# Fourier channels of the last prompt rows ahead of three products of the preceding rows, and the mixing steps with them

## The chip, the cores and the metric

The kernel runs on one core of a Trainium2 chip. The metric is the device time in microseconds of one execution. PE is TensorE, ACT is ScalarE, DVE is VectorE, POOL is GpSimd, SP is SyncE, which here only issues DMA transfers.

## The reference

One layer of a bidirectional encoder over a prompt of 2048 rows and a sample of 256, both with d_model 1024, each with a memory of 256 rows:

```python
h = rmsnorm(x, g_mix)
proj = h @ w_in                      # [q 512 | k 128 | v 128 | fourier 256 | memory q 256]
q, k, v, uf, qm = jnp.split(proj, [o1, o2, o3, o4], axis=-1)
y_attn = window_gqa_attention(q, k, v, sinks)      # |t-s| <= 128, ALiBi, sink
y_four = fourier_mix(uf)                           # real part of the 2-D DFT over rows and channels
y_mem = memory_cross_attention(qm, rmsnorm(mem, g_mem), w_mem_kv)
x = x + group_output_norm(y_attn, y_four, y_mem, g_grp) @ w_out
hf = rmsnorm(x, g_ffn) @ w_ff1                     # then squared ReLU, @ w_ff2, residual, final norm
```

The Fourier mixing needs all rows of a sequence, so its last part can only begin when the Fourier channels of the last prompt rows (rows 1792 to 2047) are there.

## The kernel before, in words

Float32 operands are split into a high and a low part (`hi_of` on ACT, L103; `lo_of` mostly on DVE, L106), and each product is three matmuls (L100).

**First stage: the input projection.** The rows go in nine groups of 256, x0 to x8 (x8 is the sample), with the two memory groups m0 and m1 between. A group is normalised (`norm`), transposed and split (`transposed`, tiles `hh` and `hl`), and multiplied in five products, `pj_g_mp`, of 48 matmuls each: mp 3 gives the Fourier channels, 2 the keys and values, 0, 1 and 4 the queries. Keys, values and queries are written to Kd, Vd and Qd in DRAM. Behind mp 3 comes `channel_mix`: the DFT over channels and, from x4 on, sums and differences with earlier rows. Norm and transposes of the next group stand at mp 1 and 4. `w2_work`, sums of rows of w_ff2 on POOL, is stepped in groups 2 to 6; what is left of it, and the ALiBi table (`bias_table`), come ahead of group 6.

**The mixing** is the generator `fourier()`. After a first `yield` and a setup it makes eleven tiles, in the order 0, 8, 4, 2, 6, 1, 7, 3, 5 (prompt) and 9, 10 (sample, which need x8's channels). For each tile a table `seq` of 256 KB is loaded on POOL's queue (L458), six matmuls give `po` (`spectrum`), and one step later `spread` evacuates and scales it (L497 to L508, with two POOL instructions at L134 and L135) and stores it to Y or Z in DRAM (L510): on ACT's queue up to the seventh tile, on POOL's from there. `mirror(1)` on ACT's queue and `mirror(0)` on POOL's (L486) copy Z to the mirrored rows of Y, 512 KB each. The generator is stepped by group 7 (once per product from the second on) and group 8 (twice per product).

**Second stage: attention and output projection.** Blocks of 128 rows go in pairs. SP loads the ALiBi table (L633), keys `kb` (L643), queries `qb` (L649), values `vb` (L651) of a pair, memory keys `km` (L663) and values `vm` (L668), the mixed channels `y` (L778), and the eight slabs of w_out (`wos`, L833), which ACT and DVE scale and split into `woh` (L170) and `wol` (L171). Scores `s` and `sm`, exponentials `p` (L684) and `pm` (L699), transposes `t`, `tm` and `ty`, products `ot` and `otm`, and the output projection `op` follow. Then comes the MLP, from about 545 us on.

**What sets the order.** The program is written in the order of the steps above, and a scheduler of the tile framework then orders the instructions of each engine; each engine works through its own in order. SP's transfers wait for buffers, for data in DRAM, and for the landing of an earlier transfer that used the same one of eight completion counters (ACT's and SP's queues share them). SP holds everything behind a transfer that waits. The second stage's buffers lie over those of the first: that of `vm` over the last tile's `fbig`, whose store must have landed. `wos` has three buffers, shared with `xr`, and its order among the transfers is kept as the scheduler first puts it (`keep_in_program_order`).

The lines that the change and the prediction touch:

```python
seq = fpool.tile([P, 2, 2, P], F32R, tag="seq", bufs=2, name=f"seq_{ti}")      # L457
pool.dma_start(seq, seq_d[ti])                                                  # L458
```

Of the kernel before, what the change touches and what calls it, by code (L numbers as in the profile page):

```python
# [11 lines left out]
F32 = mybir.dt.float32  # L12
F32R = mybir.dt.float32r
# [80 lines left out]
def trunk(ctx, tc, x, mem, w_in, w_mem, w_out, w1, w2, gains, g_final, sinks, ident_d, dist_d, cdft_d, seq_d, y):  # L94
# [52 lines left out]
    if True:  # L147
# [7 lines left out]
        wl0 = fpool.tile([P, 4, 512], F32R, name="wl0")  # L155
# [17 lines left out]
        def transposed(xs, name):  # L173
            hh, hl = [], []
            for kp in range(KT // 2):
# [8 lines left out]
                h = apool.tile([P, 2, 2, P], F32R, tag="hT", bufs=11, name=f"hh_{name}_{kp}")  # L184
                l = apool.tile([P, 2, 2, P], F32R, tag="hT", bufs=11, name=f"hl_{name}_{kp}")
# [196 lines left out]
        def group(g, side=None):  # L382
            it = order.index(f"x{g}")
            hh, hl = ready.pop(it)
            fetch(it + 2)
            post = None
            for mp in (3, 2, 0, 1, 4):
                if g == 1:
                    for k in {3: (0,), 2: (1, 2), 0: (3, 4), 1: (5, 6), 4: (7,)}[mp]:
                        load_wmem(k)  # L390
                if mp == 1:
                    norm_item(it + 1)
                if mp == 4:
                    transpose_item(it + 1)
                ps = psm.tile([P, 2, 256], F32, tag="m", name=f"pj_{g}_{mp}")
                for j in range(2):
                    m = 2 * mp + j
                    proj_T(ps[:, j], winc(0, m), winc(1, m), hh, hl)
                if post:
                    post()  # L400
                    post = None
                if mp == 3:
                    xg = None
                    if g >= 4:
                        xg = X1() if g == 8 else fpool.tile([P, 2, 2 * P], F32, tag="xg", bufs=1, name=f"xg_{g}")
                    u = [apool.tile([P, 2, 256], F32R, tag=f"u{c}", bufs=1, name=f"u{c}_{g}") for c in "hl"]
                    hi_of(u[0], ps)
                    lo_of(u[1], ps, u[0])
                    post = lambda u=u, xg=xg: channel_mix(g, u, xg)
                elif mp == 2:  # L410
                    vT = apool.tile([P, 256], F32, tag="vT", bufs=1, name=f"vT_{g}")
                    act.activation(vT, ps[:, 1], AF.Copy)
                    kt = apool.tile([P, 2, 2, P], F32R, tag="Ks", bufs=1, name=f"ks_{g}")
                    kps = ps[:, 0].rearrange("p (b t) -> p b t", b=2)
                    hi_of(kt[:, :, 0], kps)
                    lo_of(kt[:, :, 1], kps, kt[:, :, 0])
                    for dup in range(2):
                        for kv in range(2):
                            sp.dma_start(Kd[2 * g:2 * g + 2, dup * HD:(dup + 1) * HD, kv].rearrange("b p l t -> p b (l t)").bitcast(F32),
                                         kt[kv * HD:(kv + 1) * HD].rearrange("p b l t -> p b (l t)").bitcast(F32))  # L420
                    post = lambda vT=vT: values(g, vT)
                else:
                    q = apool.tile([P, 2, 2, 2, P], F32R, tag="Qs", bufs=2, name=f"q_{g}_{mp}")
                    qv = q.rearrange("p b j e t -> p e j b t")
                    pv = ps.rearrange("p j (b t) -> p j b t", b=2)
                    for e in range(2):
                        a = slice(e * HD, (e + 1) * HD)
                        for j in range(2):
                            act.activation(qv[a, e, j], pv[a, j], AF.Copy, scale=-0.125)
# [1084 lines left out]
```

## Time and profile before

| | |
|---|---|
| time, median of three runs | 2290.38 us (2289.64 to 2291.95) |
| the profiled execution | 2291.58 us, of it 2289.8 us span |
| PE busy in the span | 2205.5 us (96%) |
| DVE, ACT, POOL busy | 1643.4, 1020.2, 853.7 us |
| last matmul of the input projection ends | 351.66 us |
| first matmul of the last mixing tile, of the scores, of the output projection | 356.61, 360.33, 398.75 us |
| DMA from 350 to 362 us | 410 GB/s, busy share 1.05 |

The span runs from the first to the last instruction of the program; what lies around it is 1.8 us. Times inside are counted from the span's start. A row of a timeline has start and duration, engine, line, operation, output<-input, and in brackets the idle time ahead of it and what ended it. SPq, ACTq and POOLq rows are the issue of a transfer; the time to its landing is in the list of DMA issues. The clock is TensorE's granted clock, 1.00 at full speed.

### The profile page before, as it was taken

How to read it: one execution, taken by the hardware profiler on the slowest of the kernel's cores; microseconds unless marked ns; L12 is line 12 of the kernel's file. 1: busy time of each engine (PE TensorE's matmuls, PEld its weight loads, DVE VectorE, ACT ScalarE, POOL GpSimd, SP SyncE). 2: the span in 40 equal slices, each digit the busy share in tenths (PEclk: the TensorE clock that was granted, in tenths of full speed). 3: DMA queues.
4: the chain of work that ended last, by engine and by line, in shares of the span. 5: the costliest groups of instructions: out<-in, count | busy, mean ns of one | idle time of the engine just before them, and what ended most of it. 6: DMA issues, size and time to landing. Idle time of an engine off the chain costs nothing.

```text
span 2289.8 us, 35730 instructions
## 1 busy us (share of the span) xinstructions
PE 2205.5 (96%) x12464; PEld 1999.1 (87%) x12464; DVE 1643.4 (72%) x2962; ACT 1020.2 (45%) x2382; POOL 853.7 (37%) x821
## 2 busy tenths in 40 slices
PE   7999997999999989999999999999999999999997
PEld 7999996888888869889989889899988989999995
DVE  7334467776676758898898876877768876766688
ACT  6333357776667755444444433232224343323223
POOL 3555032014100047887786561411331421111143
PEclk9999998999999999999999999999999999999999
DMA  9987339345544368776677767856798676556563
GB/s 300 320 294 278 99 111 340 127 143 165 166 142 141 106 247 280 264 266 231 227 243 245 272 214 253 270 184 194 253 333 286 189 263 192 188 186 187 193 228 136
DMA packets 213415, 501.15 MB, mean 219 GB/s; under 512 B 20819, under 2 KB 66019, under 8 KB 210931
## 3 DMA queue, kind: packets, MB, share of 16 engines
q1 hardware_dynamic: 199872, 456.20, 59.9%
q0 software_dynamic: 10096, 39.04, 4.7%
q10 hardware_dynamic: 3267, 3.62, 0.5%
q8 instruction: 98, 1.61, 0.3%
q14 instruction: 82, 0.67, 0.1%
HBM read 345.17 MB, written 154.53 MB: 218 GB/s over the span
## 4 chain that ended last, share of the span: by engine, by line
PE 66%; DVE 6%; DMA 5%; POOL 3%; issue 2%; ACT 2%; SPq 0%; ACTq 0%; POOLq 0%; DVEq 0%
PE y L100 24%; PE op L100 8%; PE pc L100 7%; PE pa L100 7%; PE pb L100 7%; PE pd L100 4%; PE ot L100 2%; PE s L100 1%; PE t L707 1%; DMA w1s<-W1D 1%; DVE XTl L106 1%; PE yl L100 1%; DVE acc L333 1%; DMA Xn<-xr 1%; PE sm L100 1%
## 5 line engine op out<-in xcount | busy, mean ns | idle before, releaser
L100 PE MATMUL y<-w2l,ah 128*128 128x512 f32 x966 | 379.0, 392 | 5.9 <-POOL w2l L106 3.4
L100 PE MATMUL y<-w2h,al 128*128 128x512 f32 x966 | 378.8, 393 | 0.0
L100 PE MATMUL y<-w2h,ah 128*128 128x512 f32 x966 | 343.5, 393 | 1.6 <-DVE acc L336 0.9
L103 ACT ACTIVATE ah<-m 128x384 fp32r<-128x384 f32 x238 | 124.6, 524 | 491.0 <-PE y L100 485.0
L106 DVE TENSOR_TENSOR al<-m,ah 128x384 fp32r<-128x384 f32 x238 | 164.8, 693 | 156.0 <-ACT ah L103 154.2
L333 DVE TENSOR_TENSOR acc<-acc,y 128x512 f32<-128x512 f32 x378 | 240.2, 680 | 29.4 <-PE y L100 27.8
L100 PE MATMUL pc<-XTh,w1s 128*128 128x384 f32 x768 | 221.2, 341 | 10.1 <-DMA w1s<-W1D 5.4
L100 PE MATMUL pa<-XTh,w1s 128*128 128x384 f32 x768 | 219.2, 336 | 2.1 <-ACT m L1156 1.1
L100 PE MATMUL pb<-XTh,w1s 128*128 128x384 f32 x768 | 217.6, 336 | 0.9 <-DVE m L333 0.8
L100 PEld LDWEIGHTS y<-w2h,al 128*128 128x128 f32 x966 | 181.5, 188 | 30.1
L100 PEld LDWEIGHTS y<-w2l,ah 128*128 128x128 f32 x966 | 181.6, 188 | 29.6 <-POOL w2l L106 6.2
L100 PE MATMUL pj<-hl_x,winh 128*128 128x256 f32 x720 | 206.2, 288 | 0.0
L100 PEld LDWEIGHTS y<-w2h,ah 128*128 128x128 f32 x966 | 181.1, 188 | 26.3 <-DVE acc L333 1.7
L100 PE MATMUL pj<-hh_x,winl 128*128 128x256 f32 x720 | 204.0, 285 | 0.0
L100 PE MATMUL pj<-hh_x,winh 128*128 128x256 f32 x720 | 201.3, 287 | 1.1 <-ACT hh_x L103 1.1
L103 ACT ACTIVATE w2h<-w 128x512 fp32r<-128x512 f32 x322 | 198.5, 617 | 3.3 <-DMA w1s<-W1D 2.1
L106 POOL TENSOR_TENSOR w2l<-w,w2h 128x512 fp32r<-128x512 f32 x112 | 169.7, 1522 | 71.5 <-ACT w2h L103 69.4
L1028 POOL TENSOR_TENSOR ms<-m,m 128x384 f32<-128x384 f32 x48 | 59.1, 1231 | 297.1 <-DVE m L1135 215.6
L1135 DVE SCALAR_TENSOR_TENSOR m<-m 128x384 f32<-128x384 f32 x192 | 151.5, 789 | 19.3 <-ACT m L1162 17.1
L106 DVE TENSOR_TENSOR w2l<-w,w2h 128x512 fp32r<-128x512 f32 x210 | 162.0, 771 | 3.7 <-DMA W2D<-w2l 3.7
L100 PEld LDWEIGHTS pc<-XTh,w1s 128*128 128x128 f32 x768 | 143.5, 191 | 20.8 <-DMA w1s<-W1D 6.6
L100 PEld LDWEIGHTS pa<-XTh,w1s 128*128 128x128 f32 x768 | 141.3, 188 | 11.7 <-ACT m L1156 1.4
(272 smaller groups left out, 5428.2 us busy)
## 6 DMA issues: line engine op xcount, KB each, us to landing
w1s<-W1D SPq DMA_DIRECT2D x217, 512.0 KB, 4.0
W1D<-w1s SPq DMA_DIRECT2D x112, 512.0 KB, 4.0
w<-in_w_dram SPq DMA_DIRECT2D x206, 256.0 KB, 4.0
w<-W2T SPq DMA_DIRECT2D x184, 256.0 KB, 3.7
w2r<-in_w_dram SPq DMA_DIRECT2D x16, 1024.0 KB, 7.8
W2T<-w2r POOLq DMA_DIRECT2D x16, 1024.0 KB, 6.8
XTl<-Xn SPq DMA_DIRECT2D x21, 768.0 KB, 7.2
qb<-Qd SPq DMA_DIRECT2D x18, 768.0 KB, 6.8
```

The source lines that it names most:

```text
L100: pe.matmul(out, lhsT, rhs, start=start, stop=stop, skip_group_check=more)
L103: act.activation(out, src, AF.Copy, scale=scale)
L106: (eng or dve).tensor_tensor(out=out, in0=src, in1=hi.bitcast(F32), op=ALU.subtract)
L333: TT(out=o, in0=a, in1=b, op=ALU.add)
L707: pe.transpose(t[:, j], p[:, j * P:(j + 1) * P], ident)
L1028: pool.tensor_tensor(out=o, in0=a, in1=b, op=op)
L1135: dve.scalar_tensor_tensor(out=r, in0=r, scalar=0.0, in1=r, op0=ALU.max, op1=ALU.mult)
```

## The change

The product mp 3 of x7 is computed right behind mp 3 and 2 of x6, ahead of x6's 0, 1 and 4; norm and transposes of x7 come earlier, at x6's mp 3 and 2. From there on the mixing generator is stepped once per product, through x6's last three and x7's other four, then twice per product in x8. For this, `group` is split into `begin` and `part`; x7's four `hh` tiles go to a buffer of their own (it had been w_mem's `wl0`, with its later uses ended), `hT` has 12 buffers for 11, and the `seq` tables lie in turn in `seq` (one buffer for two) and in `xg`'s buffer. The ALiBi table and the rest of `w2_work` come behind x6's mp 3 and not ahead of x6.

```diff
-        wl0 = fpool.tile([P, 4, 512], F32R, name="wl0")
+        def spare(name):
+            return fpool.tile([P, 4, 512], F32R, tag="wl0", bufs=1, name=name)
+
+        wl0 = spare("wl0")
...
+            hs = spare("hh_x7") if name == "x7" else None
...
-                h = apool.tile([P, 2, 2, P], F32R, tag="hT", bufs=11, name=f"hh_{name}_{kp}")
-                l = apool.tile([P, 2, 2, P], F32R, tag="hT", bufs=11, name=f"hl_{name}_{kp}")
+                h = (apool.tile([P, 2, 2, P], F32R, tag="hT", bufs=12, name=f"hh_{name}_{kp}") if hs is None
+                     else hs[:, kp].rearrange("p (j b t) -> p j b t", j=2, b=2))
+                l = apool.tile([P, 2, 2, P], F32R, tag="hT", bufs=12, name=f"hl_{name}_{kp}")
...
+        def part(g, mp, side=None):
+            it = order.index(f"x{g}")
+            hh, hl = rows[g]
+            if g == 1:
+                for k in {3: (0,), 2: (1, 2), 0: (3, 4), 1: (5, 6), 4: (7,)}[mp]:
+                    load_wmem(k)
+            if mp == (3 if g == 6 else 1):
+                norm_item(it + 1)
+            if mp == (2 if g == 6 else 4):
+                transpose_item(it + 1)
+            ps = psm.tile([P, 2, 256], F32, tag="m", name=f"pj_{g}_{mp}")
+            for j in range(2):
+                m = 2 * mp + j
+                proj_T(ps[:, j], winc(0, m), winc(1, m), hh, hl)
+            if todo:
+                todo.pop()()
+            if mp == 3:
+                xg = None
...
+                todo.append(lambda: channel_mix(g, u, xg))
...
+            if 2 <= g < 6 or (g, mp) == (6, 3):
+                next(w2_work, None)
+                next(w2_work, None)
+            if side is not None:
+                for _ in range(2 if g == 8 else 1):
+                    next(side, None)
+
+        def group(g):
+            begin(g)
             for mp in (3, 2, 0, 1, 4):
...
-                if 2 <= g < 7:
-                    next(w2_work, None)
-                    next(w2_work, None)
-                if side is not None and not (g == 7 and mp == 3):
-                    next(side, None)
-                    if g == 8:
-                        next(side, None)
...
-            seq = fpool.tile([P, 2, 2, P], F32R, tag="seq", bufs=2, name=f"seq_{ti}")
+            seq = fpool.tile([P, 2, 2, P], F32R, tag="xg" if turn[0] % 2 else "seq", bufs=1, name=f"seq_{ti}")
...
-            elif g < 7:
+            elif g < 6:
                 if g == 3:
                     fe, fab, ffg = f8("fe"), f8("fab"), f8("ffg")
-                if g == 6:
-                    for _ in w2_work:
-                        pass
-                    bias_table()
                 group(g)
         side = fourier()
-        group(7, side)
-        group(8, side)
+        begin(6)
+        part(6, 3)
+        for _ in w2_work:
+            pass
+        bias_table()
+        part(6, 2)
+
+        begin(7)
+        part(7, 3)
+        for g, mps in ((6, (0, 1, 4)), (7, (2, 0, 1, 4))):
+            for mp in mps:
+                part(g, mp, side)
+        begin(8)
+        for mp in (3, 2, 0, 1, 4):
+            part(8, mp, side)
         for _ in side:
             pass
```

The scheduler turns this into another order on each engine. PE at the end of the products, before: `pj_4` is the last product of x8, `po_4313` is tile 10, `s` the first scores.

```order
L100 MATMUL pj_4_4343<-hh_x_3_3743,winh_220 128x256
L100 MATMUL pj_4_4343<-hl_x_3_3744,winh_220 128x256
L100 MATMUL pj_4_4343<-hh_x_3_3743,winl_221 128x256
L100 MATMUL po_4313<-Mh_4309,seq_4307 128x2x66
L100 MATMUL po_4313<-Ml_4310,seq_4307 128x2x66
L100 MATMUL po_4313<-Mh_4309,seq_4307 128x2x66
L100 MATMUL po_4313<-Mh_4309,seq_4307 128x2x62
L100 MATMUL po_4313<-Ml_4310,seq_4307 128x2x62
L100 MATMUL po_4313<-Mh_4309,seq_4307 128x2x62
L100 MATMUL s_0_4470<-kb_4458,qb_4461 128x256 x2
L100 MATMUL s_1_4526<-kb_4458,qb_4461 128x256 x2
```

After, the same tile (`po_4251`) at its new place, behind the transposes of x8's values; `pj_1` is the last but one product of x8.

```order
L100 MATMUL pj_0_4178<-hl_x_3_3833,winh_224 128x256
L100 MATMUL pj_0_4178<-hh_x_3_3832,winl_225 128x256
L380 MATMUL pv_4228<-ident,vT_4108 128x128 x2
L100 MATMUL po_4251<-Mh_4247,seq_4245 128x2x66
L100 MATMUL po_4251<-Ml_4248,seq_4245 128x2x66
L100 MATMUL po_4251<-Mh_4247,seq_4245 128x2x66
L100 MATMUL po_4251<-Mh_4247,seq_4245 128x2x62
L100 MATMUL po_4251<-Ml_4248,seq_4245 128x2x62
L100 MATMUL po_4251<-Mh_4247,seq_4245 128x2x62
L100 MATMUL pj_1_4281<-hh_x_0_3805,winl_223 128x256
L100 MATMUL pj_1_4281<-hh_x_0_3805,winh_222 128x256
```

Tile 10 moved from the end of the products to the start of the last but one; two products now follow it.

SP from the first value block to the fourth slab of w_out, before (`kb_4617`, `qb_4620` and `vb_4619` belong to the second pair of blocks):

```order
L651 DMA vb_4460<-Vd 128x3x256
L649 DMA qb_4465<-Qd 128x1536
L663 DMA km_4468<-Kmd 128x2048
L833 DMA wos_4492<-in_w_out_dram 128x1024
L833 DMA wos_4496<-in_w_out_dram 128x1024
L833 DMA wos_4500<-in_w_out_dram 128x1024
L668 DMA vm_4524<-Vmd 128x1024
L643 DMA kb_4617<-Kd 128x4x512
L649 DMA qb_4620<-Qd 128x1536
L651 DMA vb_4619<-Vd 128x4x256
L778 DMA y_4668<-Yd_72 128x256
L833 DMA wos_4504<-in_w_out_dram 128x1024
```

After (`kb_4614`, `qb_4617` and `vb_4616` are those of the second pair):

```order
L672 DMA vb_4457<-Vd 128x3x256
L670 DMA qb_4462<-Qd 128x1536
L684 DMA km_4465<-Kmd 128x2048
L689 DMA vm_4521<-Vmd 128x1024
L664 DMA kb_4614<-Kd 128x4x512
L670 DMA qb_4617<-Qd 128x1536
L672 DMA vb_4616<-Vd 128x4x256
L854 DMA wos_4489<-in_w_out_dram 128x1024
L854 DMA wos_4493<-in_w_out_dram 128x1024
L854 DMA wos_4497<-in_w_out_dram 128x1024
L799 DMA y_4665<-Yd_72 128x256
L854 DMA wos_4501<-in_w_out_dram 128x1024
```

The first three slabs moved behind `vm` and the three loads of the second pair.

ACT ahead of the first slab, before (`pth` are evacuated transposes of the exponentials):

```order
L684 ACTIVATE p_5_4553,stats_4464<-p_5_4553,stats_4464 128x256
L103 ACTIVATE pth_4_4613<-t_4_4610 128x2x128
L684 ACTIVATE p_6_4566,stats_4464<-p_6_4566,stats_4464 128x256
L103 ACTIVATE pth_4_4613<-t_5_4637 128x2x128
L684 ACTIVATE p_7_4577,stats_4464<-p_7_4577,stats_4464 128x256
L762 ACTIVATE stats_4464<-stats_4464 128x4
L103 ACTIVATE pth_4_4613<-t_6_4652 128x2x128
L170 ACTIVATE woh_4490<-wos_4492,gain 128x1024
L699 ACTIVATE pm_0_4586,stats_4464<-sm_0_4585,stats_4464 128x256
L729 ACTIVATE ots_0_4662<-ot_0_4657 128x512
```

After:

```order
L103 ACTIVATE pth_0_4556<-t_2_4577 128x2x128
L103 ACTIVATE pth_0_4556<-t_3_4592 128x2x128
L720 ACTIVATE pm_0_4583,stats_4461<-sm_0_4582,stats_4461 128x256
L103 ACTIVATE pth_4_4610<-t_4_4607 128x2x128
L705 ACTIVATE p_7_4574,stats_4461<-p_7_4574,stats_4461 128x256
L103 ACTIVATE pth_4_4610<-t_5_4634 128x2x128
L173 ACTIVATE woh_4487<-wos_4489,gain 128x1024
L783 ACTIVATE stats_4461<-stats_4461 128x4
L720 ACTIVATE pm_0_4583,stats_4464<-sm_0_4582,stats_4464 128x256
L173 ACTIVATE woh_4485<-wos_4493,gain 128x1024
```

The first `woh` stands among the same kinds of rows in both, with one exponential of the memory heads (`pm`) now ahead of it.

More of the change, by code (lines that the diff above doesn't have):

```diff
@@ L380, in values, with begin @@
                          vt.rearrange("p b v l d -> p b (v l d)").bitcast(F32))
-        def group(g, side=None):
+        rows, todo = {}, []
+        def begin(g):
             it = order.index(f"x{g}")
-            hh, hl = ready.pop(it)
+            rows[g] = ready.pop(it)
             fetch(it + 2)
-            post = None
-            for mp in (3, 2, 0, 1, 4):
[L388 to L429, printed above, removed]
-                    for e in range(2):
-                        a = slice(e * HD, (e + 1) * HD)
-                        o = slice((1 - e) * HD, (2 - e) * HD)
-                        for j in range(2):
-                            dve.scalar_tensor_tensor(out=qv[o, e, j], in0=pv[a, j], scalar=-0.125,
-                                                     in1=qv[a, e, j].bitcast(F32), op0=ALU.mult, op1=ALU.subtract)
-                    h0 = {0: 0, 1: 4, 4: 8}[mp]
-                    (pool if g == 8 else sp).dma_start(
-                        Qd[2 * g:2 * g + 2, :, h0:h0 + 4].rearrange("b p h t -> p b (h t)").bitcast(F32),
-                        q.rearrange("p b j e t -> p b (j e t)").bitcast(F32))
-                if 2 <= g < 7:
-                    next(w2_work, None)
-                    next(w2_work, None)
-                if side is not None and not (g == 7 and mp == 3):
-                    next(side, None)
-                    if g == 8:
-                        next(side, None)
@@ L448, in trunk @@
+        def group(g):
+            begin(g)
+            for mp in (3, 2, 0, 1, 4):
+                part(g, mp)
         fbig, turn, place_of = [], [0], {}
```

35 lines of the change are left out of this document (added).

## The prediction

> **What bounds the kernel now.** First the page. TensorE (PE) is busy almost all the time, so what a change in the order is worth must be looked for in the few places where PE is not busy.
>
> ```profile
> PE 2205.5 (96%) x12464; PEld 1999.1 (87%) x12464; DVE 1643.4 (72%) x2962; ACT 1020.2 (45%) x2382; POOL 853.7 (37%) x821
> ```
>
> The stretches around the change (start:end, length, busy us of each engine, granted clock, DMA share, GB/s) show where they are.
>
> ```profile
> 230.00:300.00 70.00, 70.00 (x592) 70.00 (x591) 28.83 (x58) 22.11 (x53) 2.96 (x8) 1.00 0.30 91
> 350.00:362.00 12.00, 4.68 (x25) 4.06 (x25) 4.80 (x18) 4.57 (x17) 5.79 (x12) 0.77 1.05 410
> 362.00:372.00 10.00, 7.93 (x41) 6.24 (x40) 7.37 (x30) 8.71 (x31) 2.42 (x4) 0.77 0.92 346
> 372.00:382.00 10.00, 9.24 (x42) 7.67 (x43) 8.05 (x17) 7.90 (x24) 0.00 (x0) 0.66 0.93 340
> 382.00:396.00 14.00, 10.66 (x64) 8.77 (x64) 13.56 (x39) 13.88 (x36) 0.74 (x2) 0.93 0.90 331
> 400.00:540.00 140.00, 138.10 (x830) 120.32 (x829) 102.65 (x278) 102.34 (x293) 22.41 (x41) 1.00 0.42 138
> ```
>
> The products are bound by PE without a gap: 70.00 of 70 us in the first row. From 400 on PE is the bound again (138.10 of 140). In between lie 50 us in which it is not: first the DMA is full (share 1.05), then ScalarE (ACT) is busy 13.88 of 14 us. The PE timeline gives the first gap.
>
> ```profile
> 351.38 0.28 PE L100 MATMUL pj<-hh_x,winl 128*128 128x256 f32 x1
> 356.61 0.45 PE L100 MATMUL po<-Mh,seq 128*128 128x132 f32 x1 [4.95 <-DMA seq<-in_seq_dram]
> 360.33 1.19 PE L100 MATMUL s<-kb,qb 128*128 128x256 f32 x4 [2.21 <-DMA qb<-Qd]
> ```
>
> The last product ends at 351.66. Then PE waits 4.95 us for the table of the last mixing tile, multiplies it, and waits 2.21 us for the first query block. The chain of waits says what follows, read here to the first matmul of the output projection:
>
> ```profile
> 348.38 8.09 DMA seq<-in_seq_dram
> ...
> 363.17 0.59 ACT p L684 x2
> ...
> 369.92 0.44 ACT woh L170
> ...
> 379.54 6.28 DMA wos<-in_w_out_dram
> ...
> 391.85 1.29 DVE wol L171
> ...
> 398.75 0.47 PE op L100 x2
> ```
>
> So before the output projection can start, ACT must split eight slabs of w_out (woh), among the exponentials. In this stretch the time is decided on ACT, not on PE.
>
> **The change, part by part.** *The work.* Nothing is added or removed: the same products, mixing tiles and splits. The x7 Fourier product moves ahead of three x6 products, and the mixing steps start three products earlier, so the six matmuls of the last tile (po of tile 10) now stand ahead of two whole products, 96 matmuls at 0.12 us (the spacing of the pj rows), 11.5 us.
>
> *The early part.* The norms of x4 to x7 move a little against the rest. One small wait of before, for a normalised row block, should go; its row:
>
> ```profile
> 214.01 0.44 PE L183 MATMUL tp_x<-ident,x 128*128 128x128 f32 x2 [1.33 <-DVE x L167]
> ```
>
> New small waits may come: tile 8's table now waits for a buffer shared with xg_7, and the mirror copy on ACT's queue stands ahead of the last split of x8. The gain is at most 1.33; a loss is bounded by two waits of that size, 2.7. I take -0.6 (from -1.3 to +2.0).
>
> *The end of the products.* The 4.95 us wait goes. Products end at 351.66 + 0.7 (six matmuls now inside, at no more than 0.12 each) = 352.4. If tile 10's table (8.09 us in the row above) is still late, PE waits inside the products: its buffer is released by tile 5, some 35 product matmuls and tile 9's own six, about 5 us, ahead of po, so up to 3.1 us. What is late next is the first query block. Its loads and those behind it, from the SP timeline and the list of DMA issues between 343 and 375 us (count, KB each, median us to landing):
>
> ```profile
> 343.21 0.41 SPq L633 DMA_DIRECT2D bias<-Bd  x1
> 343.71 0.41 SPq L643 DMA_DIRECT2D kb<-Kd  x1
> 348.75 0.33 SPq L649 DMA_DIRECT2D qb<-Qd  x1
> 354.78 0.51 SPq L663 DMA_DIRECT2D km<-Kmd  x1
> 356.37 3.17 SPq L833 DMA_DIRECT2D wos<-in_w_out_dram  x3
> 370.18 0.33 SPq L668 DMA_DIRECT2D vm<-Vmd  x1
> 379.12 0.32 SPq L778 DMA_DIRECT2D y<-Yd  x1
> 379.54 1.32 SPq L833 DMA_DIRECT2D wos<-in_w_out_dram  x3
> ```
>
> ```profile
> Qd<-q POOLq DMA_DIRECT2D x3, 512.0 KB, 8.2
> wos<-in_w_out_dram SPq DMA_DIRECT2D x3, 512.0 KB, 12.6
> km<-Kmd SPq DMA_DIRECT2D x1, 1024.0 KB, 11.7
> kb<-Kd SPq DMA_DIRECT2D x1, 768.0 KB, 14.7
> Yd<-Zd POOLq DMA_DIRECT2D x1, 512.0 KB, 12.4
> Vd<-vs SPq DMA_DIRECT2D x1, 256.0 KB, 6.1
> ```
>
> SP works in order behind the Vd write of x8, which stays after its product, so bias goes at about 344, much as before. The query block's DMA waited in before until the first mirror copy, which used the same one of SP's and ACT's eight completion counters, had landed (348.75); that copy is now early, so it goes at about 345.2 and, at the 11.6 us it took (348.75 to 360.33), lands at about 357. The exponentials, which began at 363.17 behind the spread of tile 10, could begin near 359. That would be the gain, some 4 us, if nothing else held ACT.
>
> *What SP does next.* Something else does. In before vm and everything behind it stood until 370.18, because vm's buffer was freed by the store of tile 10, issued here:
>
> ```profile
> 363.56 0.62 POOL L510 DMA_DIRECT2D Yd<-fbig  x1 [0.84 <-ACT fbig L508]
> ```
>
> The scheduler had put the first three slabs of w_out in front of that wait, so they went at 356.37 and the first landed 12.6 later, at 369.0; ACT came to it at 369.92 and did not wait. Now the store comes some 17 us earlier, and the order on SP is vm, kb_2, qb_2, vb_2 (the second pair of blocks) and only then wos_0. By their shapes these four are 512 + 1024 + 768 + 512 = 2816 KB, and in before the transfers of one queue landed in the order of issue (kb 358.4, qb 360.3, km 366.5, wos 369.0). ACT works in order too: its first woh stands behind 16 rows from the first exponential on (17 before, 6.75 us from 363.17), and queued behind it are the exponentials, the copies and the sums that PE and VectorE need. So when wos_0 lands decides when all of them go on.
>
> The price comes from the bytes. What the DMA moved, in the same columns as above, ahead of and after the end of the products:
>
> ```profile
> 343.20:369.00 25.80, 17.56 (x114) 15.86 (x113) 13.80 (x53) 14.69 (x56) 11.07 (x21) 0.80 1.02 377
> 351.00:369.00 18.00, 9.76 (x48) 8.06 (x47) 8.73 (x37) 10.17 (x39) 7.48 (x14) 0.72 1.04 414
> ```
>
> Before, from bias to the landing of wos_0: 25.8 us at 377 GB/s, 9.73 MB. By the issues, in KB: SP 5248 up to wos_0 (Vd 256, bias 768, kb 768, two qb 1536, vb 384, km 1024, wos 512), about half of the two slabs behind it (512), GpSimd (POOL) 1536 of Qd, 768 of mixing stores and 256 of the last table, ACT 256: 8576 KB or 8.78 MB. So about 0.95 MB was left over from issues before 343.2. After: SP 5248 + 2816 = 8064, POOL 2560 (Qd 1536, the last stores 512, the mirror copy 512): 10624 KB or 10.88 MB. With half of that leftover it is 11.4 MB. At 377 GB/s that takes 30.2 us from 343.2: wos_0 lands at 373.4. Ends: without leftover at 414 GB/s, 26.3 us, 369.5; with all of it at 346 (the row 362 to 372), 34.2 us, 377.4. I take 373, nearest to the row that covers the whole stretch: ACT's first woh begins 3.1 us later than in before (from -0.4 to +7.5), after waiting since about 359 + 6.75 = 366, and the 4 us won at the front are eaten there with 3 more.
>
> [...]
>
> *After the first slab.* From there to the second operand of the output projection ACT has the same work as before, eight woh and two yth among it, but the slabs 3 to 5 come sooner: they had stood behind y_0, which waited for the mirror copy (12.4 us in its row) until 379.12, and the chain shows 6.28 us of waiting for them. ACT was idle 10.00 - 7.90 = 2.1 us in the row 372 to 382. So at most 2.1 goes; against it woh 6 and 7 now stand ahead of the first yth, up to 2.6 (two at 1.29, the chain's row for the same shape on VectorE) if their slabs are late. I take -1.0 (from -2.1 to +2.6).
>
> *From 400 on.* PE is bound there, and its work is the same, so a shift of the start of the output projection (398.75) goes through to the end at its full size.
>
> **Sum**: -0.6 + 3.1 - 1.0 = +1.5 on the profiled execution's 2291.58 (span 2289.8). Its time is 1.2 over the median 2290.38 of three runs, so against the median 2291.9. 0.2% of this time is 4.6 us, about what its measurement can tell from no change; +1.5 is inside. A wait inside the products (3.1) costs nothing, since ACT stands at woh some 7 us anyway.
>
> **The rivals.** *Faster, 2284.6.* The wait of 4.95 us leaves the path and the slab takes its place only in part: ACT comes to woh at 366 and finds wos_0 there. Then the 4.2 us at the front (363.17 to 359) stay won: -0.6 - 4.2 - 1.0 = -5.8. It decides from a landing at 366.9 (-3.0 - 0.6 - 1.0 = -4.6). For it: 414 GB/s were moved where nothing stood still, a slab is read from an input that no other transfer touches, and that transfers land in the order of issue is seen here on five of them only. Against it: 10.88 MB by 366.9 need 459 GB/s from 343.2, more than any row above.
>
> *Slower, 2296.5.* The second pair lands as slowly as the rows from 362 to 396 moved bytes (331 to 346 GB/s), and ACT waits at woh until 377.4: +7.5 - 0.6 = +6.9, 2297.3 less the idle that goes, about 2296.5. It decides from a landing at about 376.1: 6.2 - 0.6 - 1.0 = 4.6. For it: the first 8 us of the stretch are no faster,
>
> ```profile
> 343.20:351.00 7.80, 7.80 (x68) 7.80 (x67) 5.07 (x17) 4.52 (x18) 3.59 (x8) 1.00 0.97 291
> ```
>
> with small packets of the mirror copy in them, and there is such a copy in this stretch again. Against it: later the gaps were those of a blocked SP, which go.
>
> *The clock.* A second gap of some 7 us on PE, at woh, may bring a second stretch of low clock: the two rows from 350 to 372, with the gap of before and behind it, have 0.77. If PE were the bound behind woh, 10 us at 0.77 would lose 2.3 us: 2294.2, no change still. For it: 372 to 382 has PE busy 9.24 of 10 us at 0.66. Against it: ACT's 13.88 of 14 behind that. [...]
>
> *The change doesn't do what it says.* The last table waits for its buffer and po stands in the products as long as it stood behind them, 4.95: the products end at 356.6, the query block is there, ACT still comes to woh before the slab does. The time is the same as in the forecast.
>
> **How the numbers follow.** The forecast has 0.43, the clock 0.03 and the change that does nothing 0.04, all within 0.2%: same 0.50. Faster 0.24: no rate carries it, but errors of the three terms can add up on that side, and the order of landing is open. Slower 0.26. The range takes in nearly all of the faster rival, from 2285.0, and the slower one with a us more, to 2297.5; about 0.1 is left out on each side.
>
> **What would show it.** Right: po of tile 10 with a wait under 3 us and two products behind it; the first s by 359; SP's wos behind vb_2; the first woh beginning at 371 to 376 with a wait of several us for DMA wos, PE and VectorE idle with it; later no wait for slabs 3 to 5; first op at 399 to 402. Wrong: a first woh without a wait, or an op before 395, or a bound in the products before 350 that has grown by more than 2 us.

## The result, and the profile after

| | before | after |
|---|---|---|
| time, median of 6 runs each | 2289.18 us (2288.08 to 2291.95) | 2305.23 us (2301.99 to 2307.94) |
| ratio, 95% interval | | 1.0073 (1.0063 to 1.0083) |
| the profiled execution, its span | 2291.58, 2289.8 us | 2306.12, 2304.3 us |

The change makes the kernel slower by 0.73%, some 16.7 us, and the predicted range ended at 2297.5. (The ratio, here and below, is not the quotient of the two medians and can differ from it by a tenth of a per cent. Where an effect is given in us below, it is the ratio less one, times 2289.)

The engines' busy times on the page say that the work is the same, with PE busy 3.2 us longer than before for as many matmuls:

```profile
PE 2208.7 (96%) x12464; PEld 2001.7 (87%) x12464; DVE 1644.2 (71%) x2962; ACT 1020.9 (44%) x2382; POOL 850.5 (37%) x821
```

So of the 14.5 us between the two spans some 11 are waiting, and the 3.2 go with a lower granted clock (mean 0.986 in this execution, 0.988 in that of before). Three points of the PE timeline split it: the end of the last `pj`, and the starts of the first and the last `op` (us).

| | before | after | difference |
|---|---|---|---|
| last product of the input projection ends | 351.66 | 359.65 | +8.0 |
| from there to the first `op` | 46.84 | 52.73 | +5.9 |
| from the first `op` to the last | 436.28 | 439.97 | +3.7 |
| from there to the end | 1455.0 | 1452.0 | -3.1 |

(The first `op` of before begins at 398.50; the 398.75 of the prediction is a merged row of the chain. The -3.1 is not the change's: in e8 below, the changed kernel again, this stretch is 1455.1.)

The stretches of after, in the columns of the prediction's rows:

```profile
230.00:300.00 70.00, 70.00 (x593) 70.00 (x592) 35.42 (x79) 24.17 (x59) 5.30 (x10) 1.00 0.33 105
350.00:362.00 12.00, 9.65 (x81) 9.45 (x79) 3.69 (x12) 4.12 (x12) 5.21 (x8) 1.00 0.87 293
362.00:372.00 10.00, 5.66 (x22) 4.86 (x22) 4.11 (x19) 4.13 (x16) 0.73 (x1) 0.66 1.05 402
372.00:382.00 10.00, 5.86 (x23) 4.91 (x23) 3.84 (x12) 2.82 (x10) 0.00 (x0) 0.66 1.02 389
382.00:396.00 14.00, 9.45 (x38) 7.75 (x38) 10.15 (x17) 12.02 (x27) 0.00 (x0) 0.63 0.54 176
```

The first row still has PE without a gap: where the products and mixing steps were moved, nothing is lost. In the third and fourth row ACT is busy 4.13 and 2.82 of 10 us, where before it was 8.71 and 7.90, and the DMA is full (1.05, 1.02). PE's timeline shows what it stood for:

```profile
359.37 0.28 PE L100 MATMUL pj<-hh_x,winl 128*128 128x256 f32 x1
365.29 1.20 PE L100 MATMUL s<-kb,qb 128*128 128x256 f32 x4 [5.64 <-DMA qb<-Qd]
375.29 0.98 PE L100 MATMUL sm<-km,qb 128*128 128x256 f32 x3 [4.18 <-DMA km<-Kmd]
385.47 1.22 PE L100 MATMUL sm<-km,qb 128*128 128x256 f32 x4 [3.48 <-ACT pm L720]
```

The wait for the last table (4.95 before) is gone, and two new ones stand behind the scores: for the memory keys `km`, and for ACT. On ACT it looks so (two rows of its timeline):

```profile
378.06 0.39 ACT L103 ACTIVATE pth<-t 128x256 fp32r<-128x256 f32 x1 [5.23 <-PE t L728]
383.72 1.15 ACT L173 ACTIVATE woh<-wos,gain 128x1024 fp32r<-128x1024 f32 x1 [3.58 <-DMA wos<-in_w_out_dram]
```

PE and ACT wait in turn: 5.23 us of ACT behind PE's wait for `km`, then 3.58 for the slab, behind which PE gets its 3.48. The chain of waits gives nearly all of it to one slab, and a later piece to another:

```profile
367.74 15.96 DMA wos<-in_w_out_dram
383.72 1.15 ACT woh L173
...
393.97 5.02 DMA wos<-in_w_out_dram
```

And SP's timeline has the order that the prediction read, at a later time (at `vm` it still stands 5.0 us for the store of the last tile):

```profile
351.37 0.40 SPq L654 DMA_DIRECT2D bias<-Bd  x1
...
355.05 0.79 SPq L684 DMA_DIRECT2D km<-Kmd  x1
361.11 0.32 SPq L689 DMA_DIRECT2D vm<-Vmd  x1
...
367.74 7.31 SPq L854 DMA_DIRECT2D wos<-in_w_out_dram  x3
```

That leaves the largest item, +8.0 at the end of the products. The transposes of the values (`pv`, in each group) tell when it came (PE timeline, first `pv` of the group, us):

| | x0 | x1 | x2 | x3 | x5 | x8 |
|---|---|---|---|---|---|---|
| before | 35.29 | 70.10 | 116.44 | 170.36 | 236.76 | 338.55 |
| after | 35.53 | 74.37 | 124.83 | 176.06 | 244.62 | 347.34 |

Nearly all of it is early: 8.4 us at x2 (where the order on PE differs too), 5.7 at x3 and 7.9 at x5, while the first product that the change moved starts at 272.23. Two stretches of before and then of after:

```profile
51.00:54.00 3.00, 3.00 (x27) 3.00 (x27) 3.00 (x4) 2.20 (x6) 2.53 (x3) 1.00 0.00 0
54.00:57.00 3.00, 3.00 (x27) 3.00 (x26) 2.35 (x6) 0.60 (x1) 0.00 (x0) 1.00 0.90 283
84.00:100.00 16.00, 15.81 (x135) 15.81 (x136) 9.12 (x17) 5.23 (x11) 8.94 (x9) 1.00 0.92 301
```

```profile
51.00:54.00 3.00, 0.91 (x7) 0.91 (x8) 2.94 (x4) 1.08 (x4) 2.63 (x3) 0.94 0.23 26
54.00:57.00 3.00, 3.00 (x16) 3.00 (x16) 1.88 (x5) 0.38 (x1) 0.36 (x1) 0.50 0.99 400
84.00:100.00 16.00, 12.42 (x89) 11.80 (x89) 7.13 (x11) 3.58 (x8) 11.26 (x12) 0.89 0.86 316
```

PE loses 2.1 of 3 us, and then runs at half clock: 16 matmuls in the time of 27. Over the whole time up to the end of the products, before and after:

```profile
0.00:351.66 351.66, 331.44 (x2714) 328.38 (x2714) 168.44 (x349) 146.45 (x362) 143.50 (x182) 0.99 0.70 235
0.00:359.65 359.65, 336.04 (x2720) 332.36 (x2720) 169.37 (x353) 149.54 (x372) 147.27 (x193) 0.98 0.69 235
```

PE is idle for 20.2 us before and 23.6 after. Half the clock is granted for two stretches of 3.41 us before (from 127.72 and 137.97) and for four after (from 53.64, 91.19, 142.39 and 224.31); each costs 1.7 us of full speed. So of the +8.0, 3.4 are more waiting and 3.4 the clock that falls behind the waits; the rest has the last tile's six matmuls in it, which now stand inside (x2720 for x2714). The gap's row, before:

```profile
50.93 0.66 PE L183 MATMUL tp_x<-ident,x 128*128 128x128 f32 x4 [0.55 <-DVE hl_x L106]
```

And after, with one of the same kind from the second stretch:

```profile
53.09 0.66 PE L187 MATMUL tp_x<-ident,x 128*128 128x128 f32 x4 [2.22 <-DVE hl_x L106]
90.71 0.36 PE L100 MATMUL vm<-wmh,hh_m 128*128 128x256 f32 x1 [2.06 <-DVE q L442]
```

DVE is late there because its order is another. Rows of its order there, equal instructions joined and the rows numbered, before (`wml` are splits of w_mem, `hl_x_0` to `hl_x_3` the low parts of group x1, which PE's transposes and products wait for):

```
26 L167 TENSOR_SCALAR x_1_332<-x_1_332,st_x_1_541 128x1024
27 L171 SCALAR_TENSOR_TENSOR wml_845<-wms,gain,wmh_844 128x512
28 L106 TENSOR_TENSOR hl_x_0_611<-tp_x_0_605,hh_x_0_610 128x512
29 L171 SCALAR_TENSOR_TENSOR wml_845<-wms,gain,wmh_844 128x512
30 L106 TENSOR_TENSOR hl_x_1_620<-tp_x_1_614,hh_x_1_619 128x512
```

After:

```
27 L170 TENSOR_SCALAR x_1_332<-x_1_332,st_x_1_541 128x1024
28 L174 SCALAR_TENSOR_TENSOR wml_845<-wms,gain,wmh_844 128x512 x2
29 L106 TENSOR_TENSOR hl_x_0_611<-tp_x_0_605,hh_x_0_610 128x512
30 L106 TENSOR_TENSOR hl_x_1_620<-tp_x_1_614,hh_x_1_619 128x512
31 L442 SCALAR_TENSOR_TENSOR q_4_690<-pj_4_641,q_4_690 64x2x128 x4
```

Two more splits now stand ahead of `hl_x_0` (the last two ahead of it take 3.43 us on DVE's timeline, from 48.89), and four scalings of a product's queries ahead of `hl_x_2`. The program writes all of them in the same order as before.

### The profile page after: what moved, and what is told of

Same layout as the page of the kernel before. It is cut to its first block, busy times and chain, and to the rows that moved or that the text cites. A ratio compares the mean times of both kernels' runs of the same rounds, so it can differ in the third digit from the quotient of the medians.

```text
span 2304.3 us, 35695 instructions
## 1 busy us (share of the span) xinstructions
PE 2208.7 (96%) x12464; PEld 2001.7 (87%) x12464; DVE 1644.2 (71%) x2962; ACT 1020.9 (44%) x2382; POOL 850.5 (37%) x821
## 4 chain that ended last, share of the span: by engine, by line
PE 75%; DVE 8%; DMA 7%; POOL 4%; issue 3%; ACT 2%; SPq 0%; POOLq 0%; ACTq 0%; DVEq 0%
PE y L100 23%; PE pj L100 9%; PE op L100 7%; PE pc L100 7%; PE pb L100 7%; PE pa L100 7%; PE pd L100 4%; DMA w1s<-W1D 2%; PE ot L100 2%; PE s L100 1%; PE t L728 1%; DVE acc L338 1%; DVE XTl L106 1%; DMA wos<-in_w_out_dram 1%; DMA X2d<-xr 1%
## 5 line engine op out<-in xcount | busy, mean ns | idle before, releaser
L338 DVE TENSOR_TENSOR acc<-acc,y 128x512 f32<-128x512 f32 x378 | 240.1, 679 | 30.2 <-PE y L100 28.6
```

The lines of the kernel that those rows point to most:

```text
L338: TT(out=o, in0=a, in1=b, op=ALU.add)
```

## The experiments

Two questions: which edit of the change reorders the first 150 us, and what holds the stretch behind the products. Twelve kernels were run on four chips (e1 to e4, e5 to e8, e9 and e10, e11 and e12 share one); effects are against the kernel before, run beside them on the same chip. The intervals are 2 to 4 us wide on either side, so a difference of less than that between two kernels shows nothing. "Early order" is that of PE's first 1200 instructions: only two occur, that of before and that of the changed kernel, which differ in some 300 of them.

| kernel | median us (runs) | ratio (95%) | effect us | early order | products end | first op |
|---|---|---|---|---|---|---|
| e1 buffers only | 2300.17 (5) | 1.0053 (1.0041 to 1.0066) | +12.1 | changed | 356.64 | 405.33 |
| e2 old tables | 2285.16 (11) | 0.9984 (0.9976 to 0.9993) | -3.7 | before's | 355.64 | 393.58 |
| e3 slabs first | 2298.15 (6) | 1.0044 (1.0028 to 1.0059) | +10.1 | changed | 358.03 | 403.96 |
| e4 e2 and e3 | 2288.24 (11) | 0.9998 (0.9988 to 1.0007) | -0.5 | before's | 352.95 | 395.60 |
| e5 unread load | 2305.03 (6) | 1.0071 (1.0060 to 1.0083) | +16.3 | before's | 350.51 | 402.08 |
| e6 11 buffers | 2292.11 (12) | 1.0020 (1.0007 to 1.0033) | +4.6 | changed | 357.37 | 397.14 |
| e7 e1 and unread load | 2291.07 (12) | 1.0011 (1.0002 to 1.0021) | +2.5 | before's | 359.1 | 400.98 |
| e8 after again | 2304.56 (6) | 1.0068 (1.0053 to 1.0083) | +15.6 | changed | 359.55 | 413.20 |
| e9 splits later | 2302.35 (6) | 1.0074 (1.0055 to 1.0093) | +16.9 | changed | 355.96 | 403.67 |
| e10 e5 and e9 | 2290.48 (12) | 1.0022 (1.0011 to 1.0034) | +5.0 | before's | 350.85 | 398.75 |
| e11 e10, copy later | 2286.36 (11) | 0.9994 (0.9983 to 1.0006) | -1.4 | before's | 350.09 | 394.55 |
| e12 after, copy later | 2300.94 (5) | 1.0048 (1.0034 to 1.0062) | +11.0 | changed | 356.78 | 407.23 |

In e7 the last tile stands inside the products with a wait of 4.5 us for its table; without it they would end by 354.7. Leaving it out, the products end at 350.1 to 355.6 in the six kernels with before's early order (mean 352.0, before among them) and at 356.0 to 359.7 in the seven with the changed one (mean 357.7). The six are granted 0.98 or 0.99 of the clock from 0 to 150 us and 1.00 from 150 to 240, the seven 0.97 or 0.98 and then 0.98 or 1.00. In stretches of 3.41 us at half the clock, the length measured in before and after, that is one or two for the six and three or four for the seven: about half of the 5.7 us between the means.

**e1, the buffers alone.** The kernel before with the change's two edits of buffers and nothing else: no product and no mixing step is moved.

```diff
-                h = apool.tile([P, 2, 2, P], F32R, tag="hT", bufs=11, name=f"hh_{name}_{kp}")
+                h = apool.tile([P, 2, 2, P], F32R, tag="hT", bufs=12, name=f"hh_{name}_{kp}")
...
-            seq = fpool.tile([P, 2, 2, P], F32R, tag="seq", bufs=2, name=f"seq_{ti}")
+            seq = fpool.tile([P, 2, 2, P], F32R, tag="xg" if turn[0] % 2 else "seq", bufs=1, name=f"seq_{ti}")
```

> The kernel before with only the two buffer edits of the change: hT has 12 buffers, and the mixing tables lie in turn in one seq buffer and in xg's. The order of the program is that of before. Theory: with one table buffer less, the second table is no longer loaded at the start, and the scheduler then puts VectorE's and ScalarE's work of x1, m0 and x5 in another order; this makes the early loss, so the products end 7 to 8 us later than in before (359 to 360), the rest is as before: 2296 to 2297.5. Rival: the early loss comes from the x7 product, norm and transposes that were moved, or from luck of the clock; then the products end as before and the time is 2288.5 to 2290.

Slower by 12.1 us. PE's waits up to 425 us (total, times, longest) have both of after's rows again:

```profile
PE tp_x L183 <- DVE hl_x L106: 2.9, 3, 2.2
...
PE vm L100 <- DVE q L434: 2.1, 1, 2.1
```

So the edit of buffers by itself makes a kernel slower, without anything that the change is named for. It is more than the theory said (2296 to 2297.5), and less of it is early: in the profile the products end 5.0 us later than in before, not 7 to 8, and the time from the first `op` to the last is 441.5 us for 436.3. There PE waits 3.0 for ACT's `pth`, 1.4 for `ytl` and 1.1 for `xr`; up to 545 us its waits behind the first `op` are 6.6 us, 2.0 in before.

**e2, the old tables.** The changed kernel with before's buffers: `seq` has its two buffers again, `hT` its eleven.

> The changed kernel with the two table buffers of before and hT's 11; the moved product and the earlier mixing steps stay. Theory: the early stage is that of before, the products end at 352 to 353, the slabs of w_out still wait behind the second pair of blocks and ACT waits for the first of them, 8 us or more: 2297 to 2298.5. Rival (early loss from the moved work): products end at 359 as in the changed kernel, 2304 to 2306.

Faster than both kernels, by 3.7 us against before (1.6 to 5.5), and 12 below what was expected: the slab was to be waited for, and it isn't. ACT's first split:

```profile
382.02 1.15 ACT L173 ACTIVATE woh<-wos,gain 128x1024 fp32r<-128x1024 f32 x1
```

The early order is before's. Behind the products the scheduler also came out otherwise: the first `woh` stands so much later on ACT that the slab has landed (no wait in the row), and the first `sm` later on PE, so that `km` is not waited for. The products end 4.0 us later than in before (355.64); the gain is all between there and the first `op`, 37.9 us for 46.8. So the moved work with the old buffers is 3.7 us faster as the scheduler happened to order it; how much of that is the earlier mixing, and how much the late order, no run separates.

**e3, the slabs first.** The changed kernel with its first three slabs kept ahead of `vm` and the second pair on SP, as in before.

```diff
-            for k in range(KT):
+            load_out(range(3))
...
                     pairs[b0 + 2] = load_pair(b0 + 2)
+                    if b0 == 0:
+                        load_out(range(3, KT))
```

The loads of `vm` and the second pair are kept in program order with them (`keep_in_program_order`).

> The changed kernel with the first three slabs of w_out issued ahead of vm and of the second pair's loads, as in before. Theory: the first woh no longer waits for them, the output projection starts about 6 to 8 us sooner, 2297 to 2299.5; the products still end at 359.6. Rival: the DMA has too much to bring in any order (the memory keys were late too, 4.2 us), and the gain is below 2 us: 2303 to 2306.

10.1 us slower than before (6.4 to 13.5), as expected, and 5.5 less than the changed kernel run again on another chip (e8, 12.1 to 19.0). ACT's first `woh` starts at 378.63 without a wait; PE still stands for `km`, 4.9 us. The order on SP is a part of the loss, not the whole: the products end at 358.03, and from the first `op` to the last it is 441.0 us, as long as in e1.

**e4, e2 and e3 together.**

> Both: the table buffers of before and the slabs first. Theory: the two losses are independent and add up, so the time is 2305.2 less 7.5 less 6 to 8, that is 2289.5 to 2292, and if the wait of 4.95 us that the change took away then counts, down to 2285. Rival (one loss only, or the DMA as a whole): 2297 or more.

No better than e2, which did not wait for the slabs either, and within its interval (-2.7 to +1.6) no faster than before. The time lies in what the expectation allowed ("down to 2285"), but with e2 as fast the two losses are not independent.

**e5, an unread load.** The changed kernel with a load into `xg`'s buffer at the start, at the place where before loads its second table. Nothing reads it.

```diff
+        pre = fpool.tile([P, 2, 2, P], F32R, tag="xg", bufs=1, name="pre")
+        pool.dma_start(pre, seq_d[8])
```

> The changed kernel with one load more: at the start POOL loads 256 KB of the table for tile 8 into xg's buffer, which nobody reads. It stands where the kernel before loads its second table, and with it all engines have the order of before up to x5. ACT's first woh stays as early as in the changed kernel, and the slabs behind the second pair. Theory: the missing load only reorders the early stage, worth 5 to 8 us at the products' end, and the wait of ACT at its first woh stays: 2297 to 2300. Rival 1: the reordered early stage is nearly the whole loss (buffers alone cost 12.7): 2291 to 2293. Rival 2: the order of the early stage is not what costs, and a load that nobody reads cannot help: 2304 to 2307.

The early order is before's to the row, and the products end 9.1 us sooner than in after. But the time stays: +16.3. The expectation (2297 to 2300) is missed; the time is that of rival 2, though not for its reason, since the early loss did go. PE's waits from 340 to 545 us, and ACT's first split:

```profile
PE sm L100 <- DMA km<-Kmd: 5.2, 1, 5.2
...
PE ot L100 <- ACT pth L103: 2.7, 1, 2.7
PE op L100 <- DVE ytl L106: 1.5, 1, 1.5
```

```profile
374.49 1.15 ACT L173 ACTIVATE woh<-wos,gain 128x1024 fp32r<-128x1024 f32 x1 [3.61 <-DMA wos<-in_w_out_dram]
```

The waits for `km` and the slab are those of after, moved 9 us ahead, and others (the last two rows of the waits) follow behind the first `op`. The profile is 10.0 us longer than that of before: -1.2 up to the end of the products, +4.7 from there to the first `op`, +5.0 from the first `op` to the last, +1.4 behind. The waits behind the first `op` are those of e1 (6.8 us up to 545). The execution shown is the shortest of six and the median is 3.4 us over it; of the others only the granted clock is recorded, 0.985 to 0.988 with 0.987 here.

**e6, eleven buffers.** The changed kernel with `hT` back at 11, the tables as changed.

> The changed kernel with 11 buffers for hT and not 12, tables as changed (one in xg's buffer). The early order is the changed one on PE up to x4, the first woh stands some 25 rows later on ACT. Theory: the early loss stays and ACT no longer waits at the first woh, so 2285.2 (old tables and 11 buffers) plus 5 to 8: 2290 to 2293. Rival 1 (early order is nearly all): 2296 to 2299. Rival 2 (buffers of hT decide): 2285 to 2287.

The time is as expected (2290 to 2293). The early order stays the changed one, so it is the tables' buffers that set it. Yet the time is only 4.6 over before: on ACT the first `woh` comes later (384.80 us, no wait), and PE waits for no `km`. One buffer more or less moved the late order, by 11 us of time.

**e7, e1 with the unread load.**

> The kernel before with the two buffer edits of the change, as the run that had 2300.17, and the same unread load at the start. The order is that of before up to x5 and nearly that of before behind it. Theory: the loss of 12.7 came with the order that the scheduler makes without this load, not from the smaller buffers as such: 2286 to 2290. Rival: the tables now come later and share a buffer, and that is what costs: 2296 to 2300.

+2.5, where e1 has +12.1: a transfer that nothing reads takes 9.6 us off (the theory's 2286 to 2290 is missed by 1). In the profiles, which are 13.7 apart, 8.5 of it lie between the first `op` and the last: 432.9 us, 441.5 in e1. PE's wait of 2.9 is back at

```profile
PE tp_x L183 <- DVE hl_x L106: 0.5, 1, 0.5
```

**e8, the changed kernel again**, so that e5 to e7 have it on their own chip.

> The changed kernel again, beside the other three on one chip: 2302 to 2308, products' end between 356 and 360.

+15.6, the result's size, with the products' end and the first `op` within a us of it.

**e9, the splits later.** The changed kernel with the slabs' loads and splits written 12 steps later in the second stage.

```diff
-            if n == 0:
+            if n == 12:
                 open_out()
+            if n == 0:
                 load_mem_v(0)
```

> The changed kernel with the loading and splitting of w_out written twelve units later in the attention loop. All engines have the changed kernel's order up to the attention; on SP the first slabs stand even further back, behind y_0 and the fourth query block as well, and on ACT the first woh stands 36 rows behind the first exponential and not 16. Theory: what costs is that ACT, in order, stands at its first woh until the slab has landed; with the row later ACT no longer waits, though the slab comes later, and the time falls by 8 to 13 us: 2291 to 2296.5. Rival: the bytes ahead of the slab and the late slab are what costs, wherever ACT's row stands; then the time is that of the changed kernel or more, 2304 to 2308.

A miss: +16.9 (12.6 to 21.3; by the medians +14.4), no better than the changed kernel. ACT no longer waits for a slab, but PE still does for `km`:

```profile
385.71 1.17 ACT L173 ACTIVATE woh<-wos,gain 128x1024 fp32r<-128x1024 f32 x1
```

```profile
PE sm L100 <- DMA km<-Kmd: 5.8, 1, 5.8
```

In its profile the stretch from the products' end to the last `op` is 7.9 us shorter than in after (484.8 against 492.7), which the ratio doesn't show.

**e10, e5 and e9 together.**

> The same twelve units, and the unread table load at the start, with which the early order is that of before. Theory: both losses gone, the time is that of the run with old tables and 11 buffers (2285.2), 2284 to 2289; products' end at 350 to 354. Rival (a third loss, from the late order behind the first output projection, where the run with the load alone waited 6.7 us): 2290 to 2296.

+5.0: 11.9 under e9 by the unread load alone, 11.3 under e5 by the later splits alone. Each of the two, alone, had moved the changed kernel by 1.3 at most. The time is at the lower end of the rival (2290 to 2296), and the theory's 2284 to 2289 is missed. What is left has `km` in it, and 2.6 us for ACT's `yth` at the first `op`:

```profile
PE sm L100 <- DMA km<-Kmd: 4.6, 1, 4.6
```

**e11, the copy later.** e10 with POOL's copy of the mirrored rows (512 KB from DRAM to DRAM) behind the last write of the queries: issued at 354.26, and not at 345.75.

```diff
                 if ti == 10:
                     spread(*waiting)
-                    mirror(0)
...
         for _ in side:
             pass
+        mirror(0)
```

> The run with the unread load and the later splits, with the last mirror copy (512 KB from Z to Y) written behind the last product's Qd on POOL's queue, which is about 9 us later; PE, DVE and SP keep their order up to there. Theory: PE stands 4.6 us at the first product of the memory heads (sm) because km, a 1 MB load, lands late beside this copy and the other traffic; with the copy later the first query block and km land 2 to 4 us sooner: 2286.5 to 2289. Rival: the copy takes nothing from the loads of another queue, or what is won at sm is lost again at y, which needs the copy: 2290 to 2292.

As expected: -1.4 (-3.9 to +1.4), 6.4 less than e10 on another chip, though `km` is issued by SP and the copy by POOL. From the issue of bias, `km` takes 23.9 us in e10 and 19.0 in e11 (341.80 to 360.82):

```profile
PE s L100 <- DMA qb<-Qd: 3.7, 1, 3.7
...
PE sm L100 <- DMA km<-Kmd: 1.8, 1, 1.8
```

**e12, the same copy in the changed kernel.**

> The changed kernel with the same copy later. Theory: the query block and km land 2 to 4 us sooner, but as many bytes stand ahead of the first slab as before, and ACT waits for it in order: 2302 to 2305, within 2.5 of the changed kernel. Rival: the wait of PE for km is the larger part of the late loss, and the slab's is behind it: 2298 to 2301.

+11.0 (7.8 to 14.2), 4.6 under e8, which the intervals don't fully part. That is the rival's time (2298 to 2301) and not its reason. The wait for `km` falls to 1.9, and the slab takes the place of it on ACT:

```profile
380.63 1.15 ACT L173 ACTIVATE woh<-wos,gain 128x1024 fp32r<-128x1024 f32 x1 [8.37 <-DMA wos<-in_w_out_dram]
```

```profile
PE sm L100 <- ACT pm L720: 8.1, 1, 8.1
...
PE sm L100 <- DMA km<-Kmd: 1.9, 1, 1.9
```

The slab lands at 380.6, 3.1 earlier than in after; its products ended 2.9 earlier (356.78 against 359.65). So in this trace the wait for `km` in after lay in front of the slab's and cost little by itself: the sum of the two is set by the landing.

## Why the prediction was wrong, point by point

**"The early part", -0.6 (from -1.3 to +2.0): the step that failed.** It measured +8.0. The working priced waits beside the moved products and put nothing, without a reason, on the first groups, whose lines are the same (even its own bound, two waits or 2.7, is not in its range). They don't keep their order: a second table's load at the start, which before's second `seq` buffer allowed, has no place in the changed kernel, and the scheduler then orders DVE and PE otherwise from group x0 on (PE's first different row is at 28.6 us). That the edit of buffers does this is shown by e1, e6 and e2 (it comes with the tables' buffers and goes with them), and by e5 and e7 (an unread load brings the early order back). Of the 8.0, e1 has 5.0 with the buffers alone, and in e5 all of it is gone (350.51). The order of these rows could have been compared beforehand over the whole program. How the missing load turns the scheduler's choice was not followed.

This step is the largest wrong term, but it isn't the whole: e5 is without it and no faster. The edit of buffers also changes the order behind the products (e2, e6), and there the sum had only the slabs.

The prediction itself named, as what would prove it wrong, "a bound in the products before 350 that has grown by more than 2 us". It grew, but ahead of the moved products and not in them.

**"The end of the products": right in kind.** The wait of 4.95 went, the tile stands inside the products without a wait, and from their end to the first scores it is 5.64 us for 8.67. By the forecast's times (352.4, and the scores by 359) it was to be 6.6 at most.

**"What SP does next", +3.1 (from -0.4 to +7.5): right in kind, short in size.** vm, the second pair and only then the slabs; ACT waits at its first `woh`; PE and DVE idle with it. The bytes were right too, by the row of the stretch from bias to the slab:

```profile
351.40:383.70 32.30, 19.77 (x114) 17.82 (x113) 10.43 (x37) 10.50 (x36) 4.69 (x8) 0.79 0.98 359
```

32.3 us at 359 GB/s are 11.6 MB (forecast 11.4), but at 359 and not 377 GB/s: 32.3 us for 30.2. With a start 8.2 later the slab comes at 383.7 and not at 373.4. Less the later start, the term is 5.6 and not 3.1.

**A wait that the sum didn't have: `km`.** In the changed kernel `sm` stands right behind the first scores on PE, which works in order, so PE stands 4.18 us for `km` and ACT 5.23 behind it. The order around the scores on PE was not read. It stands in e3, e5, e9 and e10 too (4.9, 5.2, 5.8, 4.6) and goes in e2 and e6, where `sm` comes later. In after it is covered by the slab's wait, as far as e12 shows.

**"After the first slab", -1.0: it was 0.** From the first `woh` to the first `op`: 28.58 us before (369.92 to 398.50), 28.66 after (383.72 to 412.38). ACT waits no longer for slabs 3 to 5 (0.26 in all) but 1.63 for woh 6, the wait that the working had set against the gain (up to 2.6); its slab is the 5.02 us of the chain.

**"From 400 on", a shift at its full size: nearly.** The first `op` is 13.9 later, the last 17.6, the end 14.5. Between the first `op` and the last, 2.3 of the 3.7 us are found: PE waits 2.6 us up to 545 where it waited 2.0, and is granted half the clock once (from 470.07, 1.7 us), in before not at all up to there. The -3.1 at the end comes and goes between executions of this kernel (e8).

**The rivals.** The slower one is nearest to the truth: the slab at 377.4 was its mechanism, and of the first `op`'s delay 5.9 us are its kind; its price of 7.5 did not take in a start that is 8.2 late. "The clock" was written for a second gap behind the scores; there it is seen (0.66, 0.66, 0.63 from 362 to 396) where PE is not the bound. Where PE is the bound, at 54 us, it does cost: 16 matmuls for 27. The rival had the mechanism and looked for it in the wrong place.

**What stays open.** The unread load and the later splits are not additive: alone they do nothing for the changed kernel (e5, e9), together 11 us (e10). In the profiles each alone does gain, at the products' end in one and behind it in the other. What takes it back in e5 is between the products' end and the last `op`, with waits for `pth`, `ytl` and `xr` behind the first `op` that e1 and e3 have too; which row makes them was not found. Nor is it settled why the kernels with the changed early order are all but e6 10 us or more behind, when their products end only some 6 us later on the average.

Not tested apart is the clock. The six runs of after were granted 0.984 to 0.987 of it on the average, before's runs beside e1 to e12 mostly 0.989 to 0.991, and one thousandth of the span is 2.3 us. So up to some 10 us of the 16.7 can be speed and not waiting (3.2 of 14.5 in the two profiled executions). Up to the products' end the low clock falls behind PE's waits (in after the longest wait just ahead of the four stretches is 2.22, 2.06, 3.6 and 1.1 us), so it is taken here as their consequence; part of it lies where PE isn't the bound, and no run separates the two.

## What to carry to other kernels

A change of buffers is a change of the whole program where a scheduler sets the order: compare the order of every engine from its first instruction, not only around the edit, and price first what comes early, since here the PE-bound work passed it on (7.9 us at x5, 8.0 at the end of the products). Try the buffers alone (e1) and the idea with the old buffers (e2): here the second is 3.7 us faster than before, and the first 12 slower. And when a stall in an in-order queue is removed, list every instruction that moves up to another late transfer (here `km` and the slabs), since here the waits took one another's place (from after to e12 that for `km` went from 4.18 to 1.9 us, and that for the slab from 3.58 to 8.37).

## What the runs showed of the hardware that was not expected

- **The clock fell behind a shorter gap than the prediction had looked at.** It had read the low clock around a wait of 4.95 us on PE and expected it behind one of some 7. In after, PE waits 1.38, 0.36 and 2.22 us between 47.6 and 53.1, and is then granted 0.50 for 3.41 us (from 53.64); in before, with 1.14, 0.36 and 0.55, the clock stays at 1.00. What the two traces have in common is a grid in time: every stretch at 0.50 up to the products' end is 3.41 us long, and within a trace their starts lie whole multiples of 3.41 us apart (3 of them from 127.72 to 137.97 in before; 11, 26 and 50 from 53.64 to 91.19, 142.39 and 224.31 in after). In the 3.41 us just ahead of each, PE was busy for 0.25 and 0.40 (before), 0.34, 0.36, 0.05 and 0.46 (after) of the time. In after, PE is busy for 1.71 us of one such piece and for 1.17 of the next, and the half clock stands behind that one:

```profile
46.81:50.23 3.42, 1.71 (x14) 1.23 (x12) 3.42 (x3) 1.49 (x4) 3.05 (x4) 1.00 0.35 132
50.23:53.64 3.41, 1.17 (x8) 0.97 (x9) 3.38 (x4) 1.64 (x5) 3.14 (x2) 1.00 0.15 16
53.64:57.05 3.41, 3.41 (x19) 3.41 (x18) 2.21 (x5) 0.60 (x1) 0.62 (x1) 0.50 0.93 362
```

Which share of busy time, over which piece, brings the half clock is not shown: half busy (1.71 of 3.42) stayed at full clock here, and in before a piece busy for 0.60 (ahead of 373.49) was followed by half clock.
- **A copy on POOL's queue delayed SP's load of `km`.** With the 512 KB copy 8.5 us later, `km` lands 4.9 us sooner after the issue of bias (19.0 for 23.9, e11 and e10). The changed kernel has it again: 18.8 in e12, with the copy 12.5 us behind that issue, and 23.9 in after, with 3.2.
